# Two chunks' inner products of the SSD scan in one block on TensorE, and banks given by kind

## The chip, the cores and the metric

The kernel runs on one core of one Trainium2 chip. The metric is the device time of one execution in microseconds. Before the change three executions took 1362.30, 1364.81 and 1369.99 us; the median, 1364.81 us, is what the change is held against.

## The reference

One layer computes a gated merge of two branches: a chunked gMLP mixer and a Mamba-2 SSD mixer. The change touches only the SSD mixer. Cut to what matters, with 8 groups g of 4 heads r, chunks of 128 positions, a state of n = 128 and p = 64 channels to a head:

```python
cb     = einsum('bclgn,bcsgn->bcgls', cc, bc)
y_diag = einsum('bcgls,bcgrls,bcsgrp->bclgrp', cb, decay, xd)          # inside the chunk
states = einsum('bcsgn,bcgrs,bcsgrp->bcgrpn', bc, decay_to_end, xd)
state  = state * chunk_decay + states                                   # from chunk to chunk
y_off  = einsum('bclgn,bcgrpn,bcgrl->bclgrp', cc, prev_states, exp(a_cs))
y      = (y_diag + y_off + d_skip * x) * silu(z)
y_b    = rms_norm(y over the 256 columns of a group)
```

Around it stand a large product with `w_in` (all inputs of both branches), the products with `w_proj_a`, `w_proj_b` and `w_out`, and a last residual sum and norm. `decay` is the causal exp of sums of `dt * a`.

## The kernel before

The program has four stages: the modulation and the first columns, the products with `w_in` (to about 910 us of the profile), the SSD stage (about 910 to 1125 us), and then the products with `w_proj_b` and `w_out`. Large products run as seven half-size products with operands split in a high and a low part, type fp32r; what the SSD stage does itself is plain fp32.

The SSD stage works through 32 **steps**. A step is one group and two neighbouring chunks (256 positions); `order` lists them, two groups in turn: (0, s=0), (1, s=0), (0, s=1), (1, s=1) and so on up to s=3, then groups 2 and 3, and so on. Even steps belong to the first group of the two, odd ones to the second. For step n the methods of `Group` issue:

- `fetch`: two loads on the SP queue, `dcy` (the sums of `dt * a`, spread over partitions) and `sl` (B, C, x and z of the step).
- `mask` and `decay`: ACT makes `ea` from `dcy`, POOL masks `dcy`, ACT takes eight exps in `dcy`.
- `prep`: on TensorE (PE) two products `pc` = C·B, with transposes of B into the same bank, and four transposes of x into `px`; then on VectorE (DVE) `dcy * pc`, `xd` and `xe` from `px`; ACT copies `bn` out of `pc`.
- `front`: on PE eight **inner products** `yi` (the diagonal term: 64 columns of weights, 128 of data, each on one half of the array's columns), and one or two **state products** `sp`; on DVE the sum of state and `sp` (`st`), the two `y1` from `yi`, and for s < 3 a second `st`, which POOL prepares with `mul_state`.
- `back`: on PE `yn` (the state's term, two or four products); on DVE `ym` from it; on POOL the sum into `y1` and the product with the gate, `yz`.
- After each second step of a group the squares of `yz` are taken; a **strip**, `post2`, sums them over partitions: four products `pq` with 32 columns of weights each, whose result DVE turns into a row (`cwt` or `tri`) that goes to DRAM.

The product with `w_proj_a` (`proj_a`, tiles `pma`) is spread between the parts of a step: one `draw` is two matmuls of 128x512; DVE then makes `tha` from each finished pair of `pma` banks and `wal`, the low part of the next weights. Matmuls are pinned in program order; on DVE, ACT and POOL the chain `link` keeps the step's own work in program order, and a scheduler places the rest (`wal`, `tha`, the rows of the strips).

The loop before, for n from 2: `front(n)`, `ahead_of(n)` (decays of step n+3, `mul_state` of n+1, mask of n+4), a draw of 4 or 5, `back(n)`, `prep(n+2)`, `fetch(n+6)`. Strips that are due stand in `front` between `yi` and `sp`.

PSUM has eight banks: two under the tag `px`, six under `bk`. In this stage `bank(name)` gave every fourth tile a `px` bank, whatever it was. Two banks (four around the end of a block of `proj_a`) are held by `pma`.

Of the kernel before, what the change touches and what calls it, by code (L numbers as in the profile page):

```python
# [35 lines left out]
def hybrid_kernel(  # L36
# [53 lines left out]
    def load(dst, src):  # L90
        pin(nc.sync.dma_start(dst, src))
# [418 lines left out]
    def bank(name):  # L510

        if pairs_done:
            pairs_done.append(name)
            if len(pairs_done) % 4 == 2:
                return psum.tile([P, 512], F32, name=name, tag="px", bufs=2)
        return psum.tile([P, 512], F32, name=name, tag="bk", bufs=6)

# [51 lines left out]
    pending, pairs_done = [], []  # L569
# [519 lines left out]
    work, last, posts = [], {}, []  # L1089
# [19 lines left out]
    class Group:  # L1109


        def __init__(self, g):
            self.g, self.pre, self.st, self.yz, self.y = g, {}, None, {}, {}

        def fetch(self, s):
            g, nm = self.g, f"{self.g}_{s}"
            n = nstep[0] % NSET
            nstep[0] += 1
            pool, b = (p2r, 2) if n < 2 else (p2q, NSET - 2)
            dcy = pool.tile([P, HPG, 2, P], F32, name=f"dcy{nm}", tag="dcy", bufs=b)  # L1120
            load(dcy.rearrange("p h i l -> p (h i l)"),
                 acs_d[g, s].rearrange("h t -> (h t)").unsqueeze(0).to_broadcast([P, HPG * 256]))
            sl = pool.tile([P, 6, 256], F32, name=f"sl{nm}", tag="sl", bufs=b)
            load(sl, s_d[g][:, s])
            if n < 2:
# [44 lines left out]
            link("A", lambda: A.copy(bn, pc[:, 256:512]))  # L1170
            self.pre[s] = (sl, dcy, bn, xs[0], xs[1], ea)

        def front(self, s):

            g, nm = self.g, f"{self.g}_{s}"
            sl, dcy, bn, xd, xe, ea = self.pre[s]
            yi = bank(f"yi{nm}")
            for i in range(2):
                for h in range(HPG):
                    j, hh = h // 2, h % 2  # L1180
                    mm(yi[hh * HD : (hh + 1) * HD, j * 256 + i * P : j * 256 + (i + 1) * P],
                       xd[:, i * 256 + h * HD : i * 256 + (h + 1) * HD], dcy[:, h, i, :])
            while posts:
                p, q, sq = posts.pop(0)
                p.post2(q, sq)
            sp = bank(f"sp{nm}")
            two = s < NCH // 2 - 1
            self.sts = [self.st]
            for i in range(2 if two else 1):
                mm(sp[:, i * 256 : (i + 1) * 256], bn[:, i * P : (i + 1) * P], xe[:, i * 256 : (i + 1) * 256])  # L1190
            self.add_state(s, 0, sp)
            if two:
                self.mul_state(s, 1)
            y1 = turn(y1_r, f"y1{nm}", F32).rearrange("p (j t) -> p j t", j=2)
            for j in range(2):
                link("V", lambda: V.scalar_tensor_tensor(y1[:, j], sl[:, 2 + j], dskt[:, 2 * g + j : 2 * g + j + 1],
                                           yi[:, j * 256 : (j + 1) * 256], op0=ALU.mult, op1=ALU.add))
            self.y[s] = y1
            if two:
                self.add_state(s, 1, sp)  # L1200
# [333 lines left out]
    def draw(n):  # L1534
        for _ in range(n):
            left[0] -= next(fill, 1) is None
# [6 lines left out]
    def ahead_of(n):  # L1543

        with tc.high_priority():
            decays(n + 3)
            if n + 1 < len(order) and order[n + 1][1]:
                groups[order[n + 1][0]].mul_state(order[n + 1][1], 0)
            for _ in range(1 if n < 29 else 2):
                beside_step()  # L1550
            masks(n + 4)

    def step(n, *fs):
        for f in fs:
            item(getattr(groups[order[n][0]], f), order[n][1])

    draw(6)
    for n in range(2):
        step(n, "front")
        ahead_of(n)  # L1560
        draw(10)
    for n in range(len(order)):
        if n > 1:
            step(n, "front")
            ahead_of(n)
# [6 lines left out]
        fetch(n + 6)  # L1572
    while tasks or work or posts:
        draw(2)
        run_tasks()
        beside_step()
        while posts:
            p, q, sq = posts.pop(0)
            p.post2(q, sq)


    room.extend(ea_r[0] + [st_tag])
# [465 lines left out]
```

## Time and profile before

| | |
|---|---|
| three executions | 1362.30, 1364.81, 1369.99 us |
| span of the profiled execution, first to last instruction | 1361.7 us |
| PE busy | 1348.6 us (99%) |
| VectorE, ScalarE, GpSimd busy | 1053.0, 800.5, 195.0 us |
| SSD stage, steps | about 912 to 1112 us |

The profile is of one execution. The page gives its span and no separate time for what lies before the first and after the last instruction; the lowest of the three times is 0.6 us above this span, the median 3.1 us.

How to read the rows: a row of the timeline has start, duration, engine, line, operation, tiles (out<-in) and a count of equal instructions that follow each other; in brackets stands idle time before it and what ended it. One fp32 matmul of the program leaves two records, so eight `yi` are a row "x16". PEld is the loading of weights, which runs beside PE. The modelled ends of PE's rows overlap; what a block costs is read from the start of one to the start of the next.

### The profile page before, as it was taken

What the parts mean: (1) busy time and instruction counts of PE and PEld (TensorE: products, weight loads), DVE (VectorE), ACT (ScalarE), POOL (GpSimd) and SP (SyncE); (2) the same over time, 40 slices, a digit from 0 to 9 for tenths busy, and PEclk for the clock granted to TensorE, in tenths of its full rate; (3) what the DMA queues carried; (4) which work ended last, traced back from release to release, by engine and by line L of the source; (5) the groups of instructions that cost most, each with busy time, mean ns of one, the idle gap of its engine ahead of it and who ended that gap; (6) DMA issues with size and microseconds to landing.
All of it is one profiled execution on the core that took longest, in us unless ns stands there. A gap on an engine that the chain in (4) does not pass through costs nothing.

```text
span 1361.7 us, 20191 instructions
## 1 busy us (share of the span) xinstructions
PE 1348.6 (99%) x6943; PEld 1116.3 (82%) x6943; DVE 1053.0 (77%) x1728; ACT 800.5 (59%) x1449; POOL 195.0 (14%) x193
## 2 busy tenths in 40 slices
PE   8999999999999999999999999999999999999997
PEld 6688888888888888888888888888888888888886
DVE  4786886787777898688887788358888867959976
ACT  5763666666656665465566655486877844233443
POOL 1000000000000000000000000007798981000002
PEclk9999999999999999999999999999999999999999
DMA  9674444344345557877766765589989959888913
GB/s 279 190 244 132 147 124 124 104 129 123 94 139 155 172 188 225 257 224 235 215 193 188 241 207 184 160 289 311 307 297 314 306 199 333 317 268 319 384 40 124
DMA packets 249578, 288.65 MB, mean 212 GB/s; under 512 B 16860, under 2 KB 196484, under 8 KB 249476
## 3 DMA queue, kind: packets, MB, share of 16 engines
q1 hardware_dynamic: 174868, 203.80, 47.1%
q10 hardware_dynamic: 74544, 83.57, 17.9%
q8 instruction: 55, 0.90, 0.3%
q14 instruction: 47, 0.39, 0.1%
q0 software_dynamic: 64, 0.00, 0.0%
HBM read 199.82 MB, written 87.49 MB: 211 GB/s over the span
## 4 chain that ended last, share of the span: by engine, by line
PE 92%; DMA 4%; DVE 2%; SPq 1%; issue 0%; ACT 0%; POOL 0%; POOLq 0%; DVEq 0%; ACTq 0%
PE xcb L565 6%; PE xz L565 6%; PE xuz L565 6%; PE xx L565 6%; PE pma L82 6%; PE xg L565 6%; PE ox L1889 3%; PE yuz L565 3%; PE yx L565 3%; PE ycb L565 3%; PE vx L970 3%; PE yp L1697 3%; PE yz L565 3%; PE yg L565 3%; PE yi L82 2%; PE sp L82 2%
## 5 line engine op out<-in xcount | busy, mean ns | idle before, releaser
L1139 POOL TENSOR_SCALAR_AFFINE_SELECT dcy<-dcy 128x1024 f32<-128x1024 f32 x32 | 35.3, 1104 | 786.9 <-DMA yl<-ya_d 743.7
L1147 ACT ACTIVATE dcy<-dcy,nacs 128x128 f32<-128x128 f32 x256 | 78.3, 389 | 2.8 <-POOL dcy L1139 2.1
L1163 DVE TENSOR_TENSOR dcy<-dcy,pc 128x1024 f32<-128x1024 f32 x32 | 39.0, 1219 | 7.9 <-PE pc L85 6.4
L1245 POOL TENSOR_TENSOR yz<-y,sl 128x512 f32<-128x512 f32 x32 | 44.4, 1389 | 2.5
L82 PE MATMUL pma<-yh,wah 128*128 128x512 f32 x128 | 43.1, 418 | 0.0
L82 PE MATMUL pma<-yh,wal 128*128 128x512 f32 x128 | 42.6, 413 | 0.0
L1040 ACT ACTIVATE ac<-ac 128x1024 f32<-128x1024 f32 x32 | 33.9, 1060 | 12.7 <-DVE ac L1038 12.6
L82 PE MATMUL pma<-yl,wah 128*128 128x512 f32 x128 | 40.2, 395 | 0.0
L1135 ACT ACTIVATE ea<-dcy 64x512 f32<-64x512 f32 x64 | 39.8, 622 | 0.4
L1170 ACT COPY bn<-pc 128x256 f32<-128x256 f32 x32 | 11.9, 372 | 47.4 <-DVE dcy L1163 47.4
L1244 POOL TENSOR_TENSOR y<-y,ym 128x512 f32<-128x512 f32 (+1 forms) x32 | 37.0, 1157 | 2.1 <-DVE ym L1242 2.1
L1038 DVE SCALAR_TENSOR_TENSOR ac<-c2x,cwt,ac 128x1023 f32<-128x1023 f32 (+2 forms) x24 | 30.7, 1279 | 8.4 <-ACT ac L1036 8.3
L1038 DVE SCALAR_TENSOR_TENSOR ac<-c2cb,cwt,ac 128x1023 f32<-128x1023 f32 (+2 forms) x24 | 30.7, 1279 | 8.1 <-ACT ac L1036 7.9
L1632 DVE SCALAR_TENSOR_TENSOR yn<-yn,par,rb 128x512 f32<-128x512 f32 x32 | 24.5, 766 | 15.4 <-DMA yn<-yb_d 13.9
L1904 POOL TENSOR_TENSOR r<-r,fnw 128x512 f32<-128x512 f32 x4 | 6.1, 1530 | 204.1 <-ACT junk L1902 204.1
L82 PE MATMUL yi<-dcy,xd 128*64 128x128 f32 x512 | 35.0, 279 | 0.0
L1242 DVE TENSOR_TENSOR ym<-yn,ea 128x512 f32<-128x512 f32 (+1 forms) x32 | 19.9, 622 | 18.4 <-PE yn L82 18.3
L840 ACT CAST wbb<-wbr 128x512 fp32r<-128x512 f32 x32 | 19.8, 619 | 23.8 <-DMA wb_d<-wbb 17.4
L82 PE MATMUL sp<-xe,bn 128*128 128x256 f32 x112 | 32.7, 409 | 0.0
L82 PEld LDWEIGHTS yn<-sl,st 128*128 128x128 f32 x224 | 29.7, 191 | 2.9 <-POOL st L1208 0.4
L82 PEld LDWEIGHTS yi<-dcy,xd 128*64 128x64 f32 x512 | 27.3, 136 | 5.7 <-issue 3.2
L1038 DVE SCALAR_TENSOR_TENSOR ac<-c1cb,cwt,ac 128x1023 f32<-128x1023 f32 (+2 forms) x24 | 30.6, 1276 | 1.3 <-ACT ac L1036 1.3
(2978 smaller groups left out, 4379.1 us busy)
## 6 DMA issues: line engine op xcount, KB each, us to landing
sl<-s_d SPq DMA_DIRECT2D x32, 768.0 KB, 6.6
s_d<-ac ACTq DMA_DIRECT2D x32, 512.0 KB, 3.7
wb_d<-wbb ACTq DMA_DIRECT2D x32, 512.0 KB, 3.7
dcy<-acs_d SPq DMA_DIRECT2D x32, 512.0 KB, 5.0
av<-in_w_in_dram SPq DMA_DIRECT2D x36, 256.0 KB, 3.1
aw<-in_ada_w_dram SPq DMA_DIRECT2D x16, 512.0 KB, 5.9
wbr<-in_w_proj_b_dram SPq DMA_DIRECT2D x32, 256.0 KB, 4.8
yb_d<-yz ACTq DMA_DIRECT2D x32, 256.0 KB, 5.9
```

The source lines that it names most:

```text
L82: pin(PE.matmul(acc, l, r, start=first, stop=last))
L565: pin(PE.matmul(ps, lw[:, k * P : (k + 1) * P], r[k], start=first and n + k == 0, stop=n == 2 and k == 3, skip_group_check=not first))
L970: pin(PE.matmul(ps[pn][j], l[:, j * P : (j + 1) * P], r, start=nm in ("p1", "p5", "p2") and n + units[i][1] == 0, stop=n == 2 and k == 3, ...
L1038: V.scalar_tensor_tensor(ac[:, s:], cc[:, : S - s], conv_wt[:, 3 - s, i : i + 1], ac[:, s:], op0=ALU.mult, op1=ALU.add)
L1135: link("A", lambda: A.activation(ea[hh * HD : (hh + 1) * HD], dcy.rearrange("p (j e) i l -> p e j (i l)", e=2)[hh * HD : (hh + 1) * HD, hh ...
L1139: link("G", lambda: G.affine_select(out=d8, in_=d8, compare_op=ALU.is_ge, fill=-1e30, base=0, pattern=[[0, 2 * HPG], [1, P]], channel_mult ...
L1147: link("A", lambda: A.activation(dcy[:, h, i, :], dcy[:, h, i, :], AF.Exp, bias=sub[:, i, h : h + 1]))
L1163: link("V", lambda: V.tensor_tensor(d3, d3, pc[:, 0:256].unsqueeze(1).to_broadcast([P, HPG, 256]), op=ALU.mult))
L1244: link("G", lambda: G.tensor_add(y1[:, :, t0:], y1[:, :, t0:], m[:, :, t0:]))
L1245: link("G", lambda: G.tensor_mul(yz, y1, sl[:, 4:6]))
L1697: pin(PE.matmul(ps[j], a[:, v, js], r, start=first and n + k == 0, stop=n == 2 and k == KT - 1, skip_group_check=not first))
L1889: pin(PE.matmul(ps, a[:, tsl], b[:, cs], start=first and n + j == 0, stop=n == 2 and j == 3, skip_group_check=not first))
```

## The change

Three things are altered. The inner products become a method of their own, `inner`, and are issued for two steps at once: steps n and n+1 (n even) right before `front(n)`, behind a draw of 3; steps 0 and 1 stay single. The strips that are due stand right behind that block. The draws inside the loop become 3, 2 (3 for n=2) and 4 in place of 4 (6 for n=2) and 5. And the two `px` banks go to the tiles `px` and `pc` of `prep`, all else to the six others.

```diff
         if pairs_done:
             pairs_done.append(name)
-            if len(pairs_done) % 4 == 2:
+            if name[:2] in ("px", "pc"):
                 return psum.tile([P, 512], F32, name=name, tag="px", bufs=2)
         return psum.tile([P, 512], F32, name=name, tag="bk", bufs=6)
...
-        def front(self, s):
-
-            g, nm = self.g, f"{self.g}_{s}"
-            sl, dcy, bn, xd, xe, ea = self.pre[s]
-            yi = bank(f"yi{nm}")
+        def inner(self, s):
+
+            dcy, xd = self.pre[s][1], self.pre[s][3]
+            self.yi[s] = yi = bank(f"yi{self.g}_{s}")
             for i in range(2):
                 for h in range(HPG):
                     j, hh = h // 2, h % 2
                     mm(yi[hh * HD : (hh + 1) * HD, j * 256 + i * P : j * 256 + (i + 1) * P],
                        xd[:, i * 256 + h * HD : i * 256 + (h + 1) * HD], dcy[:, h, i, :])
-            while posts:
-                p, q, sq = posts.pop(0)
-                p.post2(q, sq)
+
+        def front(self, s):
+
+            g, nm = self.g, f"{self.g}_{s}"
+            sl, _, bn, _, xe, _ = self.pre[s]
+            yi = self.yi.pop(s)
             sp = bank(f"sp{nm}")
...
-    for n in range(len(order)):
-        if n > 1:
-            step(n, "front")
-            ahead_of(n)
-            draw(6 if n == 2 else 4 + n % 2)
+    def strips():
+        while posts:
+            p, q, sq = posts.pop(0)
+            p.post2(q, sq)
+
+    def inners(*ns):
+        with tc.high_priority():
+            for n in ns:
+                groups[order[n][0]].inner(order[n][1])
+            strips()
+
+    def behind(n):
         step(n, "back")
         if n == 1:
             draw(4)
         if n + 2 < len(order):
             step(n + 2, "prep")
         fetch(n + 6)
+
+    for n in range(2, len(order)):
+        if n % 2 == 0:
+            draw(3)
+            inners(n, n + 1)
+        step(n, "front")
+        ahead_of(n)
+        draw(4 if n % 2 else 3 if n == 2 else 2)
+        behind(n)
```

What it moves is seen best in the order of the instructions. First TensorE around steps 8 and 9 (groups 2 and 3, s=0; the names carry group and s). Before, from the transposes of step 9 through the inner products of step 8, one strip and the state product:

```order
L82 MATMUL yi2_0_9010<-dcy2_0_8685,xd2_0_8914 64x128 x8
L82 MATMUL pq1_0_9019<-yz1_0_8495,ones_140 32x128 x4
L82 MATMUL sp2_0_9026<-xe2_0_8916,bn2_0_8918 128x256 x2
L82 MATMUL pma2_0_8812<-yh30_8122,wal2_0_8563 128x512
L82 MATMUL pma2_1_8815<-yh31_8123,wal2_0_8563 128x512
```

In the changed kernel, the same place; six `pma` now stand between the transposes and this block:

```order
L82 MATMUL pma2_0_8812<-yh40_8141,wah2_1_8533 128x512
L82 MATMUL pma2_1_8815<-yh41_8142,wah2_1_8533 128x512
L82 MATMUL yi2_0_9009<-dcy2_0_8683,xd2_0_8923 64x128 x8
L82 MATMUL yi3_0_9018<-dcy3_0_8768,xd3_0_8990 64x128 x8
L82 MATMUL pq0_0_9027<-yz0_0_8465,ones_140 32x128 x4
L82 MATMUL pq1_0_9034<-yz1_0_8495,ones_140 32x128 x4
L82 MATMUL sp2_0_9041<-xe2_0_8925,bn2_0_8927 128x256 x2
```

The inner products of step 9 (`yi3_0`) have moved ahead of step 8's state product, and two strips that stood in two steps stand together.

Then VectorE, which takes its work in order, from `ym` of step 10 on. Before:

```order
L1242 TENSOR_TENSOR ym2_1_9210<-yn2_1_9205,ea2_1_8853 128x512
L1163 TENSOR_TENSOR dcy2_2_9005<-dcy2_2_9005,pc2_2_9217 128x1024
L1166 TENSOR_TENSOR xd2_2_9227<-px2_2_9216,dthq_154 128x512
L1166 TENSOR_TENSOR xe2_2_9229<-px2_2_9216,dde_155 128x512
L1400 TENSOR_TENSOR wal4_1_9381<-wa4_1_8808,wah4_1_9380 128x512
L1285 TENSOR_SCALAR cwt_148<-pq0_1_9247 128x128
L1216 TENSOR_TENSOR st_8275<-st_8275,sp3_1_9254 128x256
```

In the changed kernel:

```order
L1244 TENSOR_TENSOR ym2_1_9219<-yn2_1_9214,ea2_1_8851 128x512
L1402 TENSOR_TENSOR wal4_1_9334<-wa4_1_8808,wah4_1_9333 128x512
L1163 TENSOR_TENSOR dcy2_2_8996<-dcy2_2_8996,pc2_2_9226 128x1024
L1166 TENSOR_TENSOR xd2_2_9236<-px2_2_9225,dthq_154 128x512
L1166 TENSOR_TENSOR xe2_2_9238<-px2_2_9225,dde_155 128x512
L1218 TENSOR_TENSOR st_8275<-st_8275,sp3_1_9247 128x256
L1198 SCALAR_TENSOR_TENSOR y13_1_9252<-sl3_1_8931,dskt_151,yi3_1_9177 128x256 x2
```

Here `wal` has moved ahead of the next step's `dcy * pc`, and the strip's row has gone from this place.

Last, a piece of VectorE's order that reads the same in both: the work of step 5's `front` with the two `tha` of a finished block of `proj_a`, in the changed kernel:

```order
L1163 TENSOR_TENSOR dcy0_3_8525<-dcy0_3_8525,pc0_3_8750 128x1024
L1166 TENSOR_TENSOR xd0_3_8760<-px0_3_8749,dthq_154 128x512
L1166 TENSOR_TENSOR xe0_3_8762<-px0_3_8749,dde_155 128x512
L1218 TENSOR_TENSOR st_8275<-st_8275,sp1_2_8773 128x256
L1198 SCALAR_TENSOR_TENSOR y11_2_8778<-sl1_2_8489,dskt_151,yi1_2_8703 128x256 x2
L1508 SCALAR_TENSOR_TENSOR tha1_0_8452<-tha1_0_8452,pma1_0_8454 128x512
L1508 SCALAR_TENSOR_TENSOR tha1_1_8455<-tha1_1_8455,pma1_1_8457 128x512
L1218 TENSOR_TENSOR st22_8278<-st22_8278,sp1_2_8773 128x256
L1244 TENSOR_TENSOR ym1_2_8824<-yn1_2_8818,ea1_2_8491 128x512
L1163 TENSOR_TENSOR dcy1_3_8617<-dcy1_3_8617,pc1_3_8829 128x1024
```

What has moved against it is TensorE's order: before, the inner products of step 7, which read what the last row begins, stood behind those of step 6, a state product, five draws, `yn` and the transposes of step 8; now only three draws and the inner products of step 6 stand between.

More of the change, by code (lines that the diff above doesn't have):

```diff
@@ L1112, in __init__ @@
         def __init__(self, g):
-            self.g, self.pre, self.st, self.yz, self.y = g, {}, None, {}, {}
+            self.g, self.pre, self.st, self.yz, self.y, self.yi = g, {}, None, {}, {}, {}
         def fetch(self, s):
@@ L1555, in step @@
             item(getattr(groups[order[n][0]], f), order[n][1])
-    draw(6)
-    for n in range(2):
-        step(n, "front")
-        ahead_of(n)
-        draw(10)
-    for n in range(len(order)):
-        if n > 1:
-            step(n, "front")
-            ahead_of(n)
-            draw(6 if n == 2 else 4 + n % 2)
+    def strips():
[8 more added lines that the diff above has]
+    def behind(n):
         step(n, "back")
@@ L1572, in hybrid_kernel @@
         fetch(n + 6)
+    draw(6)
+    for n in range(2):
+        inners(n)
+        step(n, "front")
+        ahead_of(n)
+        draw(10)
+    for n in range(2):
+        behind(n)
[3 more added lines that the diff above has]
+            inners(n, n + 1)
+        step(n, "front")
+        ahead_of(n)
+        draw(4 if n % 2 else 3 if n == 2 else 2)
+        behind(n)
     while tasks or work or posts:
@@ L1576, in hybrid_kernel @@
         beside_step()
-        while posts:
-            p, q, sq = posts.pop(0)
-            p.post2(q, sq)
+        strips()
     room.extend(ea_r[0] + [st_tag])
```

## The prediction

> **What bounds the kernel now.** I read the page first: its head, the clock row and the chain that ended last.
>
> ```profile
> span 1361.7 us, 20191 instructions
> PE 1348.6 (99%) x6943; PEld 1116.3 (82%) x6943; DVE 1053.0 (77%) x1728; ACT 800.5 (59%) x1449; POOL 195.0 (14%) x193
> PEclk9999999999999999999999999999999999999999
> PE 92%; DMA 4%; DVE 2%; SPq 1%; issue 0%; ACT 0%; POOL 0%; POOLq 0%; DVEq 0%; ACTq 0%
> ```
>
> TensorE is busy 99% of the span at full clock, and 92% of the chain is TensorE. A busy PE can still hide gaps between blocks, so the stage of the change comes next: the view by windows for 930 to 1100 us (busy time of PE, PEld, DVE, ACT, POOL, then clock, DMA share and GB/s), and the view of waits in the same stretch.
>
> ```profile
> 930.00:1100.00 170.00, 170.00 (x1367) 144.87 (x1366) 143.26 (x253) 127.41 (x338) 147.22 (x143) 1.00 0.88 302
> ...
> DVE ym L1242 <- PE yn L82: 12.9, 17, 1.6
> DVE dcy L1163 <- PE pc L85: 5.7, 16, 0.5
> DVE st L1216 <- POOL st L1208: 5.7, 9, 1.3
> PEld sp L82 <- issue: 4.2, 23, 0.2
> PEld yi L82 <- issue: 2.4, 14, 0.2
> PEld pq L82 <- issue: 2.1, 12, 0.2
> ```
>
> No row there has PE waiting for another engine; VectorE waits for PE. POOL (147.22 of 170 us, 87%) and VectorE (143.26, 84%) are nearly full, though. The three last rows are the interesting ones: loading weights pauses 0.2 us for no engine, always at `yi`, `pq` and `sp`. The timeline of the weight loads shows where:
>
> ```profile
> 1010.53 0.85 PEld L82 LDWEIGHTS yi<-dcy,xd 128*64 128x64 f32 x16 [0.17 <-issue]
> 1011.55 0.16 PEld L82 LDWEIGHTS pq<-yz,ones 128*32 128x32 f32 x8 [0.17 <-issue]
> 1011.91 0.30 PEld L82 LDWEIGHTS sp<-xe,bn 128*128 128x128 f32 x2 [0.20 <-issue]
> ```
>
> The first shape of a row is the part of the array that the weights fill, and it changes at each pause: 128*128 to 128*64, to 128*32, and back. The next block waits there. The same place in PE's own timeline:
>
> ```profile
> 1008.44 1.05 PE L82 MATMUL yn<-sl,st 128*128 128x128 f32 x8
> 1009.33 0.39 PE L82 MATMUL pc<-sl 128*128 128x128 f32 x2
> ...
> 1010.22 0.38 PE L85 MATMUL px<-ident,sl 128*128 128x128 f32 x2
> 1010.53 1.09 PE L82 MATMUL yi<-dcy,xd 128*64 128x128 f32 x16
> 1011.55 0.43 PE L82 MATMUL pq<-yz,ones 128*32 128x128 f32 x8
> 1011.91 0.70 PE L82 MATMUL sp<-xe,bn 128*128 128x256 f32 x2
> ```
>
> From 1009.33 to 1010.22 eight records pass, 0.11 us each; two more end at 1010.44, and `yi` starts at 1010.53. **Entering costs 0.09 us.** Sixteen `yi` load in 0.85 us, yet `pq` starts 1.02 us after them. **Leaving costs 0.17 us.** A strip costs 0.36 us.
>
> **The change, part by part.** *Fewer entries.* Thirty steps come in 15 pairs with one entry and one exit each. `yi` is now entered from `pma` and not from `px`; the trace has that once, at step 0:
>
> ```profile
> 911.19 0.62 PE L82 MATMUL pma<-yl,wah 128*128 128x512 f32 x2
> 911.64 0.61 PE L82 MATMUL pma<-yh,wal 128*128 128x512 f32 x2
> 912.19 0.33 PE L82 MATMUL yi<-dcy,xd 128*64 128x128 f32 x2
> ```
>
> A pair of `pma` takes 0.45 us to the next, and 0.55 to `yi`: about 0.09 again. So each pair saves 0.09 + 0.17 = 0.26 us, and 15 x 0.26 = **3.9 us**. [...]
>
> *Strips together.* The order has 12 blocks of one strip in the loop before; now 4 blocks of two and 4 of one. Behind the loop the trace has two in one block:
>
> ```profile
> 1112.87 0.65 PE L82 MATMUL pq<-yz,ones 128*32 128x128 f32 x16
> 1113.44 0.50 PE L82 MATMUL pma<-yl,wah 128*128 128x512 f32 x1
> ```
>
> 0.57 us for two against 0.36 for one: the second costs 0.21, so 0.15 is saved four times, **0.6 us**. The gain on PE is 4.5 us. All else on PE is the same work in another place. `px` is now followed by `sp` at odd steps, same shape and type, at no cost.
>
> *What covers VectorE now.* Before, step n+1's `xd` had a whole step of PE work until its inner products. I lay out a pair by rows (n even, times in us from the end of the transposes of step n+1). The long leg: three draws 1.39, entry 0.09, `yi` of n at 1.48, **`yi` of n+1 at 2.33**, `sp` at 3.35. With
>
> ```profile
> 1023.68 1.13 PE L82 MATMUL sp<-xe,bn 128*128 128x256 f32 x4
> 1024.46 0.80 PE L82 MATMUL pma<-yh,wah 128*128 128x512 f32 x2
> 1025.10 0.63 PE L82 MATMUL pma<-yl,wah 128*128 128x512 f32 x2
> ```
>
> (`sp` 0.78, the first draw behind it 0.64) `yn` starts at 5.23, ends at 6.12, and the transposes of n+2 end at 7.23. The short leg from there: `sp` of n+1, four draws, `yn` from 2.81 to 3.70, transposes of n+3 until **4.81**. VectorE's part, from one step:
>
> ```profile
> 1000.93 0.41 DVE L1216 TENSOR_TENSOR st<-st,sp 128x256 f32<-128x256 f32 x1
> 1001.26 0.86 DVE L1196 SCALAR_TENSOR_TENSOR y<-sl,dskt,yi 128x256 f32<-128x256 f32 x2
> 1002.07 0.42 DVE L1216 TENSOR_TENSOR st<-st,sp 128x256 f32<-128x256 f32 x1
> 1004.04 0.69 DVE L1242 TENSOR_TENSOR ym<-yn,ea 128x512 f32<-128x512 f32 x1 [1.55 <-PE yn L82]
> 1004.98 1.22 DVE L1163 TENSOR_TENSOR dcy<-dcy,pc 128x1024 f32<-128x1024 f32 x1 [0.25 <-ACT ea L1135]
> 1006.12 0.68 DVE L1166 TENSOR_TENSOR xd<-px,dthq 128x512 f32<-128x512 f32 x1
> 1006.72 0.68 DVE L1166 TENSOR_TENSOR xe<-px,dde 128x512 f32<-128x512 f32 x1
> 1007.32 0.68 DVE L1400 TENSOR_TENSOR wal<-wa,wah 128x512 fp32r<-128x512 f32 x1
> 1007.91 0.41 DVE L1216 TENSOR_TENSOR st<-st,sp 128x256 f32<-128x256 f32 x1
> ```
>
> `dcy` starts about 0.04 behind the transposes and `xd` is done 1.82 later, at 1.86: **0.47 us ahead of the 2.33**, less the hand-over. In the short leg VectorE runs `dcy`, `xd`, `xe` until 2.38, `st` until 2.71, `y` until 3.52, `st` until 3.9, then `ym` behind `yn`, at 3.9, until 4.6; the next `dcy` is due at 4.85. So the common pair fits without a wait, with 0.25 us to spare on VectorE and some 0.3 more at `yi`. The bare cost is zero; the exceptions are:
>
> ```profile
> L1506 DVE SCALAR_TENSOR_TENSOR tha<-tha,pma x16: 673/678/687, 931.6 to 1129.7; 128x512 f32<-128x512 f32 x16
> ...
> L1285 DVE TENSOR_SCALAR cwt<-pq x8: 276/278/283, 964.1 to 1121.8; 128x128 f32<-128x128 f32 x8
> ```
>
> - Two short legs (steps 5 and 21) hold two `tha`: 1.2 us more, less 0.25 to spare, less 0.4 at `yi`: 0.5 us each, **1.0**. Behind them queue the second `st`, `ym` and `dcy`, and PE waits at the odd `yi`.
> - In the four blocks of two strips all six `bk` banks are taken (two `pma`, two `yi`, two `pq`), so `sp` needs one back: the first strip ends 0.43 us into its block, its row takes 0.28, and `sp` would stand at 0.57. With a hand-over 0.15 to 0.3 lost; I take 0.25, **1.0** in all.
> - In steps 10 and 26 two `tha` and a `wal` stand ahead of the next `dcy`, which comes 0.6 late; `st` of the odd step then ends behind 3.26, where the second half of `yn` needs it: 0.3 each, **0.6**.
> - Odd steps with s=0 need `st` at 2.81, and it ends at 2.79; with POOL's sums here and there, **0.4**.
>
> Together 3.0 us of new waits, with bounds of zero (VectorE hides it all) and 12 (0.8 in each of 15 pairs). I take 3.0, from the four places counted.
>
> *Banks by kind.* `px` and `pc` of one step now use the very banks of the step before; those come free with `xe`, 2.46 after the transposes, and ACT's `bn`, before that, and are needed at 3.70 at the earliest. Nothing, as long as VectorE is less than 1 us late.
>
> The stages behind are bound by PE and start that much earlier. The sum: 1361.7 - 4.5 + 3.0 = 1360.2 for this execution's span. The median stands 3.1 above that span and the lowest run 0.6, so I put the forecast between what the two give, 1360.8 and 1363.3, nearer the median: **1362.8 us**.
>
> **The rivals.**
>
> - *All of it is kept.* VectorE hides the exceptions as it hid them before. For: PE waits for nothing in 170 us now. Against: the cover was a step then and is 0.5 us now. 1364.8 - 4.5 = 1360.3.
> - *Slower: POOL and VectorE can't follow the short leg.* The second `st` of an odd step needs POOL's product with the state, which queues behind `y` and `yz` of the even step. The row above has VectorE waiting for it 9 times, once 1.3 us. That costs nothing now; where `dcy` comes over 0.5 us late it becomes a wait of PE at the odd `yi`. At 1.3 us late each pair loses 0.8: 15 x 0.8 - 4.5 = +7.5, 1372.3. For it speaks POOL's 87%; against it that the next long leg has 1.5 us in which VectorE catches up. [...]
> - *The gaps aren't the mode's.* If each new step's weights brought the pause, and not the change of shape, two `yi` blocks in a row would have it between them too: nothing saved, the waits stay, 1364.8 + 3.0 = 1367.8. Against it: the pauses stand at `pq` and `sp` too, always where the shape changes.
>
> **How the numbers follow.** Forecast 50%, all kept 20%, the short leg 18%, the gaps 12%. Two of the cases (70%) lie from 1360 to 1363, and the third run before was 5.2 above its median, so a median of few runs moves by some 2 us. The range, 1358.5 to 1370.0, takes in the first two cases, the gaps' and the milder half of the short leg. About 0.5%, 6.8 us, is what a measurement of this kernel can tell from no change. Faster than 1358.0 is more than PE's whole gain and needs a lucky median: 0.10. Slower than 1371.6 needs most of the short leg's price: 0.13. The rest, 0.77, is within it.
>
> **What would show it.** In the profile after: `yi` in rows of x32 with one pause ahead and one behind, 17 in place of 32; two strips in a row of x16 in the loop. Right in size, if SSD steps take 5 us less but for waits of PE at odd `yi`, at `sp` behind two strips and at `yn`, about 3 us together. Wrong, if PE waits at `yi` in most pairs (the short leg), or if `yi` x32 takes clearly over 1.87 us (the gaps).

## The result, and the profile after

| | before | changed |
|---|---|---|
| median (six executions each) | 1364.55 us | 1373.61 us |
| lowest, highest | 1362.30, 1369.99 us | 1372.13, 1376.82 us |
| span of the profiled execution | 1361.7 us | 1372.3 us |

The changed kernel is slower: the ratio is 1.0059, with a 95% interval of 1.0042 to 1.0076. The forecast of 1362.8 us and its range up to 1370.0 both missed. The medians differ by 9.1 us, the spans of the two profiled executions by 10.6; the rest of this text works with the spans, since only these executions have a trace.

The page of the changed kernel first, with the same lines that were shown of before.

```profile
span 1372.3 us, 20196 instructions
...
PE 1348.0 (98%) x6943; PEld 1115.7 (81%) x6943; DVE 1056.4 (77%) x1728; ACT 800.8 (58%) x1449; POOL 197.0 (14%) x193
...
PEclk9999999999999999999999999999999999999999
...
PE 82%; POOL 7%; issue 3%; DMA 3%; ACT 2%; SPq 1%; DVE 1%; POOLq 0%; ACTq 0%; DVEq 0%
```

PE is as busy in us as before, in a span that is 10.6 us longer: the time is idle time of PE, not more work. The chain that ended last agrees, since PE's share of it fell from 92% to 82%. Next the view by windows of 930 to 1100 us and, below it, PE's waits over the whole span (us in total, times, longest).

```profile
930.00:1100.00 170.00, 162.08 (x1290) 137.58 (x1290) 141.22 (x241) 121.30 (x321) 138.92 (x135) 1.00 0.84 288
```

```profile
PE pp L85 <- DMA pk<-in_ada_b_dram: 3.5, 1, 3.5
PE yn L82 <- DVE st L1218: 3.1, 4, 1.2
PE pq L82 <- POOL yz L1275: 1.9, 1, 1.9
PE yn L82 <- DVE y L1198: 1.5, 2, 0.8
PE yi L82 <- DVE xd L1166: 1.5, 1, 1.5
PE pma L82 <- DVE st L1218: 1.5, 1, 1.5
PE px L85 <- DVE x L359: 1.5, 2, 0.9
PE sp L82 <- DVE cwt L1287: 0.8, 4, 0.2
PE yi L82 <- ACT bn L1170: 0.6, 1, 0.6
PE yn L82 <- POOL st L1210: 0.6, 1, 0.6
```

Before, PE was busy for 170.00 of these 170 us and waited for nobody; now it is busy for 162.08. Most of its new waits name VectorE (8.4 us); 2.5 us name POOL and 0.6 ACT. Short ones do not appear as waits of PE, so I also read each block from its start to the start of the next and compared equal blocks with each other. Three starts cut the stage, and they can be read from PE's timeline: `yi` of step 4, `yi` of step 28, and the first product behind the stage, `x0p`. Before:

```profile
943.90 1.09 PE L82 MATMUL yi<-dcy,xd 128*64 128x128 f32 x16
...
1090.05 1.09 PE L82 MATMUL yi<-dcy,xd 128*64 128x128 f32 x16
...
1125.21 0.39 PE L1697 MATMUL x0p<-p1bh,p1a 128*128 128x512 f32 x1
```

The changed kernel, with its first `yi` at 911.71 (912.19 before):

```profile
911.71 1.09 PE L82 MATMUL yi<-dcy,xd 128*64 128x128 f32 x16
...
948.55 1.64 PE L82 MATMUL yi<-dcy,xd 128*64 128x128 f32 x26
...
1100.35 0.88 PE L82 MATMUL yi<-dcy,xd 128*64 128x128 f32 x12
...
1136.53 0.39 PE L1716 MATMUL x0p<-p1bh,p1a 128*128 128x512 f32 x1
```

The middle, steps 4 to 27, took 146.15 us and takes 151.80. The table has these stretches for every kernel of this study, from the first `yi` to `yi` of step 4, from there to `yi` of step 28, and from there to `x0p`. Where a pair stands at a cut, its draw ahead of the block moves a few `pma` records (0.23 us each) from one stretch to another; the numbers are put to the same count (74, 216 and 82). "Behind" is from `x0p` to the start of PE's last record.

| kernel | span | steps 0 to 3 | steps 4 to 27 | step 28 to `x0p` | behind |
|---|---|---|---|---|---|
| before | 1361.7 | 32.6 | 146.2 | 34.2 | 229.4 |
| changed | 1372.3 | 36.8 | 151.8 | 36.2 | 228.6 |
| e2_banks_alone | 1361.6 | 32.6 | 146.2 | 34.2 | 230.5 |
| e3_prep_behind | 1414.3 | 37.3 | 187.2 | 39.9 | 229.0 |
| e4_first_single | 1370.4 | 32.6 | 152.5 | 37.8 | 228.9 |
| e5_legs | 1372.0 | 37.2 | 150.8 | 36.5 | 228.8 |
| e6_sum_first | 1367.1 | 34.1 | 150.1 | 36.4 | 228.5 |
| e7_strip_banks | 1373.4 | 34.5 | 152.6 | 38.6 | 229.6 |
| e8_y_early | 1374.5 | 34.4 | 153.4 | 36.3 | 231.7 |
| e9_all | 1368.5 | 32.6 | 147.1 | 37.6 | 232.6 |
| e10_last_single | 1372.9 | 34.6 | 151.7 | 35.4 | 232.9 |
| e11_bn_behind | 1377.1 | 34.5 | 158.5 | 37.7 | 228.5 |
| e12_all_mid | 1373.0 | 32.7 | 154.8 | 37.7 | 229.6 |
| e13_all_y_late | 1376.3 | 34.1 | 156.7 | 36.9 | 230.3 |
| e14_quiet_pairs | 1364.7 | 32.6 | 146.5 | 34.3 | 233.4 |
| e15_sum_and_y | 1377.2 | 37.8 | 149.2 | 36.3 | 236.0 |
| e16_both_ends | 1364.8 | 32.6 | 147.6 | 35.2 | 231.0 |

So the 10.6 us are 4.2 at the start, 5.65 in the middle and 1.9 at the end, less 1.2 that other stages differ by. The waits themselves are larger, since the gain on PE is in these numbers: added up block by block they are 4.5, 10.4 and 2.5 us, 17.4 together, against a gain of 5.6. The middle's 10.4 are, by kind: 5.3 where an odd step's `yn` waits for the state sum `st`, 1.9 where `yn` of steps 5 and 21 waits for `y`, 1.9 at odd `yi`, 0.9 at `sp` behind strips, and 0.4 in pieces of 0.1 in blocks that began behind a wait.

The dearest place in the middle is step 11 (step 27 is its twin). This is the timeline of PE and VectorE there, with one row of POOL, from the second state sum of step 10 on.

```profile
990.86 0.41 DVE L1218 TENSOR_TENSOR st<-st,sp 128x256 f32<-128x256 f32 x1
...
991.19 0.68 DVE L1244 TENSOR_TENSOR ym<-yn,ea 128x512 f32<-128x512 f32 x1
991.21 1.03 PE L82 MATMUL sp<-xe,bn 128*128 128x256 f32 x4
991.42 1.09 POOL L1139 TENSOR_SCALAR_AFFINE_SELECT dcy<-dcy 128x1024 f32<-128x1024 f32 x1
991.79 1.26 DVE L1402 TENSOR_TENSOR wal<-wa,wah 128x512 fp32r<-128x512 f32 x1
...
992.98 1.21 DVE L1163 TENSOR_TENSOR dcy<-dcy,pc 128x1024 f32<-128x1024 f32 x1
...
993.91 0.60 PE L82 MATMUL yn<-sl,st 128*128 128x128 f32 x4
994.11 0.68 DVE L1166 TENSOR_TENSOR xd<-px,dthq 128x512 f32<-128x512 f32 x1
...
994.71 0.67 DVE L1166 TENSOR_TENSOR xe<-px,dde 128x512 f32<-128x512 f32 x1
995.31 0.41 DVE L1218 TENSOR_TENSOR st<-st,sp 128x256 f32<-128x256 f32 x1
...
995.76 0.71 PE L82 MATMUL yn<-sl,st 128*128 128x128 f32 x4 [1.25 <-DVE st L1218]
```

`sp` was done at about 992, and the sum that `yn` needs takes 0.41 us. But ahead of it in VectorE's queue stand `wal`, then `dcy`, `xd` and `xe` of step 12, whose inner products start only at 998.88. PE stands still for 1.25 us although VectorE is never idle: it works on what is not urgent.

### The profile page after: what moved, and what is told of

It is laid out like the page before. It is cut to its first block, busy times and chain, and to the rows that moved or that the text cites. A ratio compares the mean times of both kernels' runs of the same rounds, so it can differ in the third digit from the quotient of the medians.

```text
span 1372.3 us, 20196 instructions
## 1 busy us (share of the span) xinstructions
PE 1348.0 (98%) x6943; PEld 1115.7 (81%) x6943; DVE 1056.4 (77%) x1728; ACT 800.8 (58%) x1449; POOL 197.0 (14%) x193
## 4 chain that ended last, share of the span: by engine, by line
PE 82%; POOL 7%; issue 3%; DMA 3%; ACT 2%; SPq 1%; DVE 1%; POOLq 0%; ACTq 0%; DVEq 0%
PE xcb L565 6%; PE xz L565 6%; PE xuz L565 6%; PE xx L565 6%; PE xg L565 5%; PE ox L1908 3%; PE yuz L565 3%; PE yx L565 3%; PE ycb L565 3%; PE yz L565 3%; PE yp L1716 3%; PE vx L970 3%; PE yg L565 2%; PE oy L1908 2%; POOL y L1246 2%
## 5 line engine op out<-in xcount | busy, mean ns | idle before, releaser
L1139 POOL TENSOR_SCALAR_AFFINE_SELECT dcy<-dcy 128x1024 f32<-128x1024 f32 x32 | 37.8, 1182 | 784.2 <-DMA yl<-ya_d 743.7
L82 PE MATMUL pma<-yl,wah 128*128 128x512 f32 x128 | 44.1, 426 | 0.0
L1135 ACT ACTIVATE ea<-dcy 64x512 f32<-64x512 f32 x64 | 39.9, 623 | 0.6 <-DMA dcy<-acs_d 0.2
L1040 ACT ACTIVATE ac<-ac 128x1024 f32<-128x1024 f32 x32 | 33.9, 1061 | 10.8 <-DVE ac L1038 10.4
L82 PE MATMUL pma<-yh,wal 128*128 128x512 f32 x128 | 39.9, 393 | 0.0
L82 PE MATMUL yn<-sl,st 128*128 128x128 f32 x224 | 32.6, 281 | 5.6 <-DVE st L1218 3.1
```

The lines of the kernel that those rows point to most:

```text
L82: pin(PE.matmul(acc, l, r, start=first, stop=last))
L1135: link("A", lambda: A.activation(ea[hh * HD : (hh + 1) * HD], dcy.rearrange("p (j e) i l -> p e j (i l)", e=2)[hh * HD : (hh + 1) * HD, hh ...
L1139: link("G", lambda: G.affine_select(out=d8, in_=d8, compare_op=ALU.is_ge, fill=-1e30, base=0, pattern=[[0, 2 * HPG], [1, P]], channel_mult ...
```

## The experiments

The theories on record: S (the short leg, as the rival in the prediction had it), B (the banks), and from the fifth run on Q (the order in VectorE's queue), P (POOL and ACT), later A, T, L and M, each told where it is tested. Each run was one execution, but for e14. A single span is a loose measure, since 17 executions of the kernel before lie from 1361.42 to 1368.88 us; a stretch is a better one. The middle of the kernel before came out at 146.15 and 146.17 (e2), and that of the changed kernel, whose code from step 4 to step 27 is also that of e10 and e4, at 151.8, 151.7 and 152.5. So a difference of less than about 0.8 us in the middle says little.

**The banks alone.** The kernel before, with the new rule:

```diff
-            if len(pairs_done) % 4 == 2:
+            if name[:2] in ("px", "pc"):
```

> The kernel before with the banks given by kind, and nothing else of the change. Theory S (short leg: with the prep of step n+2 ahead of the front of step n+1 on VectorE, and little PE work between, PE waits for VectorE's st at the odd yn): inner products stay single, so no wait is new and the span stays at 1361.7 us, within 0.5. Theory B (banks: the six banks for all else are too few once pma holds four): PE waits 2.4 us at the first new block of proj_a, and 0.9 us at two later ones, as in the changed kernel: span 1364 to 1367 us.

Measured: span 1361.6 us, and every stretch of the stage equal to the kernel before within 0.1 us. Theory B falls: the bank rule costs nothing by itself, and the loss comes with the pairs and the strips that stand with them. A kernel with the pairs and the old rule was not run.

**The next step's preparation behind the odd step's front.**

```diff
-        if n + 2 < len(order):
+        if n + 2 < len(order) and (n < 2 or n % 2):
             step(n + 2, "prep")
...
         step(n, "front")
+        if n % 2 and n + 1 < len(order):
+            step(n + 1, "prep")
```

> The changed kernel, but for even n the prep of step n+2 is issued behind the front of step n+1, so that on VectorE st and y of the odd step stand ahead of dcy, xd and xe of step n+2. Theory S: the waits at odd yn (5.7 us in the changed kernel) and at odd yi (2.0 us) go for the most part: span 1365 to 1367 us. Theory B: the waits are for banks, the span stays at 1372 us, within 1.

Measured: 1414.3 us, a miss for both theories. The first two rows of PE's waits in that kernel, the second not a new one, say why:

```profile
PE pc L82 <- ACT bn L1170: 27.1, 11, 3.3
PE pp L85 <- DMA pk<-in_ada_b_dram: 3.5, 1, 3.5
```

The edit moved the transposes too, not only VectorE's work, so two preparations came close together and the second needed the two `px` banks while ACT had not yet emptied `pc`. It tested the banks, not the queue. The granted clock also fell nine times behind these waits, to 0.50, as told at the end.

**The first pair single, and other legs.** In e4 steps 2 and 3 are single, with draws of 6 and 4:

```diff
-        if n % 2 == 0:
+        if n < 4:
+            inners(n)
+        elif n % 2 == 0:
             draw(3)
             inners(n, n + 1)
...
-        draw(4 if n % 2 else 3 if n == 2 else 2)
+        draw(6 if n == 2 else 4 if n % 2 else 2)
```

> The changed kernel with steps 2 and 3 single as steps 0 and 1 are, pairs from step 4 on. Theory S: the 1.7 us wait at the inner products of step 3 goes, one pair's gain of 0.35 us goes too: span 1371 us. Theory B: that wait stays or moves to a bank: 1372 us or more.

In e5 one draw moves from ahead of the block into odd steps:

```diff
-            draw(3)
+            draw(2)
...
-        draw(4 if n % 2 else 3 if n == 2 else 2)
+        draw(5 if n % 2 else 3 if n == 2 else 2)
```

> The changed kernel with one draw moved from the long leg (2 in place of 3 ahead of the inner products) to the short leg (5 in place of 4). Theory S: the short leg is 0.46 us longer, which takes up to 0.46 off each wait at an odd yn (8 of them) and leaves the odd yi 0.46 less ahead of it: span 1369 to 1372 us, with the sum of the waits at yn down from 5.7 to about 3 us. Theory B: no change beyond 0.5 us.

Measured: e4 1370.4 us, near S's 1371, and e5 1372.0, which both theories allow. In e4 the first stretch is back at 32.6, all 4.2 us of it; the span fell by 1.9 only, since the middle and the end are longer there (how the end came to that is told at e9). What the pair of steps 2 and 3 ran into stands in the changed kernel's VectorE rows:

```profile
931.78 1.82 DVE L1402 TENSOR_TENSOR wal<-wa,wah 128x512 fp32r<-128x512 f32 x2
933.52 1.27 DVE L1508 SCALAR_TENSOR_TENSOR tha<-tha,pma 128x512 f32<-128x512 f32 x2
934.72 1.21 DVE L1163 TENSOR_TENSOR dcy<-dcy,pc 128x1024 f32<-128x1024 f32 x1
935.85 0.68 DVE L1166 TENSOR_TENSOR xd<-px,dthq 128x512 f32<-128x512 f32 x1
```

2.9 us of `proj_a`'s work stand ahead of step 3's `dcy`, and `yi` of step 3 waits until 936.59. The other 2.4 us of the start, steps 0 and 1, came with the execution and not with the change: kernels with the same code there (e7, e10, e11) have 34.5 us. The trace has the cause: POOL's first select of the stage took 3.52 us in the changed kernel and 3.51 in e15, the two with the whole of this loss, and 1.09 to 1.10 in the other fifteen kernels, the one before included; the 2.43 us between them are the loss (its row stands at the end of this text). e5 and e13 lose 1.2 and 1.5 us there behind a select of the usual length. In e5 the waits at odd `yn` shrink and odd `yi` waits in their place; to shift the draws only moves the wait.

**VectorE's order.** In e6 `xd` and `xe` of an even step (from step 4) are put aside in `prep` and issued by the odd step's `front` behind the first state sum:

```diff
             self.add_state(s, 0, sp)
+            while rest:
+                rest.pop(0)()
```

> The changed kernel, but on VectorE xd and xe of even steps (from step 4 on) stand behind the first state sum of the odd step before them; the rest of the order is kept. Theory Q (the order in VectorE's queue): the second half of yn of odd steps waits because the state sum stands behind dcy, xd and xe of the next step; with the sum 1.2 us earlier the waits at odd yn (5.7 us in all in the changed kernel) fall below 1.5 us, span 1372.3 - 4.2 = 1368.1, within 1. Theory P (POOL's products with the state and ACT's decays are what comes late): VectorE's order does not matter, the waits stay, span 1372.3 within 0.7.

In e7 strips use the `px` banks:

```diff
-            if name[:2] in ("px", "pc"):
+            if name[:2] in ("px", "pc", "pq"):
```

> The changed kernel, but strips take their banks from the two of px and pc. Both theories: the four waits of sp behind two strips (0.26 us each) go, and nothing else, since px and pc are free at that place: span 1372.3 - 1.1 = 1371.2, within 0.5. If the next transposes then wait for the rows of the strips, the span stays at 1372.3 or rises.

In e8 the `y` of a step is a method of its own, `diag`, and that of an odd step stands right behind the even step's front:

```diff
         step(n, "front")
+        if n % 2 == 0:
+            step(n + 1, "diag")
```

> The changed kernel, but the two y of an odd step (from step 3 on) stand on VectorE right behind the even step's front, and not in its own. Theory Q: the bank of odd yi comes free a step earlier, so yn of steps 5 and 21 no longer waits (-1.8 us); the short leg has 0.8 us less on VectorE, so dcy of the next step starts earlier and odd yi waits less (1.9 us now): span 1368.5 to 1369.5. Theory P: only the 1.8 us of the bank go, 1370.5.

e9 has these three edits and e4's.

> All of these together: single inner products for steps 2 and 3, xd and xe of even steps behind the odd step's first sum, y of odd steps early, strips in the banks of px and pc. Theory Q: 1372.3 - 1.9 - 4.2 - 1.1 - 1.8 - 1.0 = 1362.3, within 1.5, which is about the kernel before (1361.7 to 1362.7). Theory P: 1372.3 - 1.9 - 1.1 - 1.8 = 1367.5.

Measured: e6 1367.1, e7 1373.4, e8 1374.5, e9 1368.5 us. At step 11, e6 looks like this:

```profile
989.56 1.21 DVE L1165 TENSOR_TENSOR dcy<-dcy,pc 128x1024 f32<-128x1024 f32 x1
...
990.50 1.36 PE L82 MATMUL yn<-sl,st 128*128 128x128 f32 x8
990.69 0.41 DVE L1227 TENSOR_TENSOR st<-st,sp 128x256 f32<-128x256 f32 x1
991.02 0.68 DVE L1169 TENSOR_TENSOR xd<-px,dthq 128x512 f32<-128x512 f32 x1
991.62 0.67 DVE L1169 TENSOR_TENSOR xe<-px,dde 128x512 f32<-128x512 f32 x1
```

The sum comes ahead of `xd` and `xe`, and the eight records of `yn` pass in one row. In the middle the waits at odd `yn` for `st` fall from 5.3 to 0.65 us: the mechanism of theory Q is shown. But the middle got shorter by 1.7 us only, because 1.8 us come back at odd `yi` and 0.9 at the transposes, which wait for the later `xe`. Of e6's 5.2 us in the span, 2.7 stand in steps 0 to 3, mostly in what varies, so that the span came out near Q's 1368.1 in part by luck. In e7, where the span was to fall to 1371.2, no `sp` waits for a strip any more (0.9 us in the middle), yet the middle is 0.8 us longer and the end 2.5. In e8, which both theories had faster than the changed kernel, `yn` of steps 5 and 21 hardly waits any more (0.2 for 1.9), as both theories said, but the early `y` makes `ym`, the next `dcy` and the sum late, up to 2.1 us at step 11. Alone, e8 loses and e7 gains nothing; together (e9) the middle is 147.1 us, within 1 us of before.

The span of e9 does not follow, because of the end: it is nearer to P's 1367.5 than to Q's 1362.3, but for a reason that neither had. These are windows of e9 (the number ahead of the last two is PE's granted clock):

```profile
1114.00:1116.00 2.00, 1.41 (x12) 1.07 (x13) 1.44 (x1) 0.00 (x0) 1.92 (x3) 0.93 1.04 397
1116.00:1118.00 2.00, 2.00 (x6) 1.52 (x6) 0.53 (x2) 0.00 (x0) 2.00 (x2) 0.50 0.47 166
1118.00:1120.00 2.00, 2.00 (x8) 1.58 (x7) 0.00 (x0) 1.66 (x4) 1.12 (x2) 0.72 0.84 250
...
1134.00:1136.00 2.00, 2.00 (x6) 1.63 (x5) 2.00 (x4) 1.66 (x3) 0.69 (x1) 0.50 0.71 262
```

PE waited 2.03 us until 1114.59 for POOL's sum, as the changed kernel does for 1.9, and 1.9 us until 1131.5 for a strip's row. Behind both waits the granted clock fell to 0.50 for 3.4 us, which costs about 1.6 us each time (worked out at the end of this text). The same dip, to 0.50 for 3.4 us, lengthens the end of e4 (from 1121.1) and of e7 (from 1121.9).

**The end, and ACT.** In e10 steps 30 and 31 are single:

```diff
-        if n % 2 == 0:
+        if n > 29:
+            inners(n)
+        elif n % 2 == 0:
...
-        draw(4 if n % 2 else 3 if n == 2 else 2)
+        draw(4 + n % 2 if n > 29 else 4 if n % 2 else 3 if n == 2 else 2)
```

> The changed kernel, but steps 30 and 31 stay single, with the draws of before (4 and 5). Theory T (the end of the stage has its own price: the last step's sums and strips come later when step 31's front stands behind step 30's back with its inner products drawn ahead): the 2.1 us that PE waits at the strips behind the loop for POOL's sum go, less 0.35 for one pair's gain: span 1372.3 - 1.75 = 1370.5, within 0.5. If POOL is late from steps further back, the wait stays: 1372.6.

In e11 ACT's copy of `bn` of an even step (from step 4) is put aside in `prep` and issued behind the next decays:

```diff
             decays(n + 3)
+            while rest_b:
+                rest_b.pop(0)()
```

> The changed kernel, but ACT copies bn of an even step (from step 4 on) behind the decays of the odd step after it, and not ahead of them. Theory A (part of the lateness goes through ACT: bn waits for the bank that VectorE's dcy reads, the decays of the next step stand behind bn, and VectorE's next dcy waits for them): the waits at odd yi (1.95 us in all) go and those at odd yn, 5.7 us, do not grow: span 1372.3 - 2.0 = 1370.3, or lower. Theory Q alone (VectorE's queue): 1372.3 within 0.5.

e12 is e9 with both of these, and e13 is e12 without the early `y`.

> The kernel with all the edits of before together (single steps 2 and 3, state sum first, y of odd steps early, strips in the banks of px and pc), and now also steps 30 and 31 single and bn of even steps behind the decays. That kernel's stage took 217.3 us against 213.0 of the kernel before, with 3.9 us of waits at the strips and late squares behind the loop, 2.3 at odd yi and 2.3 behind the stage for a row of strips. If each wait has its own cause: 1368.5 - 3.9 - 2.3 - 2.3 = 1360.0, 1 to 2 us below the kernel before. If the waits only move on: 1364 to 1367.

> The same, but with y of odd steps in their own front again. Steps 5 and 21 then wait for their bank at yn as in the changed kernel: +1.8 us against the run before it in this job. If the early y costs as much elsewhere (its run alone was 2.2 us slower than the changed kernel), the two are equal or this one is faster.

Measured: e10 1372.9, e11 1377.1, e12 1373.0, e13 1376.3 us. In e10 the stretch at the end falls by 0.8 us (the wait for POOL's sum from 1.9 to 0.8), less than half of what theory T said, and a wait of 2.5 us for the last `tha` appears behind the stage, with a dip of the clock to 0.50. Theory A falls as a remedy: with `bn` later, PE waits at the transposes for its bank (4.9 us for `px` in e11), and e12 and e13 carry the same stall. As e3 did, it shows that the two `px` banks have to be emptied soon. Its mechanism is borne out, though: in e11 VectorE's `dcy` nowhere waits for ACT's exps any more, and the waits at `yi` of steps 11, 27 and 31 are gone (more on this in the next section). e12 missed both of its numbers by 6 us or more, and e12 and e13 do not test what they were made for. Between them e13 was to be 1.8 us slower or equal; its middle is 2.0 us longer and its span 3.3.

**Where pairs are cheap, and which edits belong together.**

In e14 six pairs are left:

```diff
-        if n % 2 == 0:
+        if n & -2 not in (8, 12, 14, 16, 24, 28):
+            inners(n)
+        elif n % 2 == 0:
...
-        draw(4 if n % 2 else 3 if n == 2 else 2)
+        draw(6 if n == 2 else 4 + n % 2 if n & -2 not in (8, 12, 14, 16, 24, 28) else 4 if n % 2 else 2)
```

> The changed kernel, but pairs only for steps 8, 12, 14, 16, 24 and 28 and their followers, where the changed kernel's PE waited least; all others single with the draws of before (6 for n=2, else 4 and 5). Theory L (each pair pays its own waits, set by what else VectorE holds at that place; a pair there does not disturb the steps around it): six pairs gain 6 x 0.35 = 2.1 us and two double strips 0.3, against waits of 0.27 twice, 0.15 three times and 0.44 once: 1361.7 - 1.0 = 1360.7 within 1, and the stage up to the last step about 1 us shorter than before. Theory M (POOL, ACT and VectorE are late on the whole; any pair brings waits, in the mean 0.82 a pair as in the changed kernel's steps 4 to 27): 1361.7 + 6 x 0.47 = 1364.5.

e15 has the edits of e6 and e8 alone, and e16 is e9 with steps 30 and 31 single.

> The changed kernel with two edits alone: xd and xe of even steps behind the odd step's first state sum, and y of odd steps early. From the inner products of step 4 to those of step 28 the kernel before takes 146.15 us, the changed kernel 151.80, the sum alone 150.06, the early y alone 153.40, and all edits together 147.1. Theory Q (VectorE's order, the two edits need each other: y has left the short leg, so that the state sum and dcy both come early): 147.5 to 148.5 in that stretch. If the strips' banks did it: 150 or more.

> All edits together as before (single steps 2 and 3, sum first, early y, strips in the banks of px and pc), and steps 30 and 31 single, without the edit of bn. Theory T (the end has its own price): the stretch from step 28 to the first product behind the stage falls from 37.6 to 35.4 us, and the span to 1368.5 - 2.2 = 1366.3; to 1363 if PE's clock does not fall behind the waits at the end either.

Measured, e14: median 1367.58 us of 12 executions against 1363.95 of 17 before, a ratio of 1.0029 with an interval of 1.0017 to 1.0040; span 1364.7. The span is M's number (1364.5), but by luck: in the stage, where M would have some 3 us more than before and L about 1 less, the middle is 146.5 us, 0.3 longer than before, and the other two stretches are as before. The waits that L listed are there again, 0.15 at steps 9, 17 and 25 and 0.45 at steps 14 and 15, and so are local to a pair's place, as L has it (these pairs bring no two strips together, so neither that gain nor those waits of L's sum come up); but even the cheap places no more than pay for themselves, since single strips now wait for POOL's sums (0.4 us at step 11). The other 4 us lie behind the stage, at a place whose code is the same in both kernels, here in PE's timeline:

```profile
1125.36 0.39 PE L1718 MATMUL x1p<-p1bh,p1a 128*128 128x512 f32 x1
1128.71 0.50 PE L1718 MATMUL x2p<-p1bh,p1a 128*128 128x512 f32 x1 [2.96 <-DVE tha L1508]
```

The bank of `x2p` was still held by `proj_a`'s last block; in the kernel before, `x2p` follows at once. Which bank falls to it seems to depend on how the banks were given out; I did not test this.

e15: the middle is 149.2 us, between the two answers. Its span of 1377.2 us, the longest but for e3's, has two other sources: the slow select at the start again, with a dip of the clock behind it (0.50 for 3.4 us), and a wait of 4.76 us at `x2p` with another (0.50 for 6.8 us), by which the part behind the stage is 6.6 us longer than before. In the middle the two edits bring 2.6 us of the 5.65, and e16, which adds the strips' banks and the ends, 1.5 more. e16 is the best of the full versions with 1364.8 us; its last stretch fell by 2.4 us, as theory T said, and the span by 3.7. No version came out below the kernel before; e16's one execution (1366.82 us) lies within the scatter of that kernel.

## Why the prediction failed, step by step

- **Fewer entries (3.9 us) and strips (0.6): right in mechanism, a little small.** The gain was 5.6 us in the stage where 4.5 was forecast. A clean pair shows it: in e9, from `yi` of step 4 to that of step 6, nothing waits:

```profile
944.06 1.97 PE L82 MATMUL yi<-dcy,xd 128*64 128x128 f32 x32
...
956.02 1.20 PE L82 MATMUL yi<-dcy,xd 128*64 128x128 f32 x18
```

That is 11.96 us. Before, from the row at 943.90 to this one, it was 12.30:

```profile
956.20 0.98 PE L82 MATMUL yi<-dcy,xd 128*64 128x128 f32 x14
```

So a pair saves 0.34 where 0.26 was forecast, 5.1 us in 15 pairs, and the four double strips bring the rest; `sp` of odd steps, now behind transposes, takes 0.68 us to the next block and not 0.78, which the working had not seen. The rival that the gaps come with each new step's weights, and not with the change of shape, falls: the 32 records pass in one row (at 944.06) with no pause between the two steps.

- **"The common pair fits without a wait": this step failed.** The working gave `st` of an odd step the end 2.71 against a need at 3.26, half a microsecond of room. It laid out one pair, with VectorE's work in a row with nothing between, at its shortest durations. Three things are not in it:
  - At s=3 (steps 7, 15 and 23) `sp` is half as long, 0.25 us and not 0.68, so `yn` comes 0.43 earlier. `dcy` starts only 0.1 us later than in other pairs there (0.5 behind step 23), and yet `yn` waits 0.3 to 0.7 for `st`.
  - At steps 3 and 19 a `wal` stands ahead of the next `dcy`, as at the listed steps 11 and 27; `dcy` starts 0.6 to 0.7 us later than in other pairs, and `yn` waits 0.4 and 0.5.
  - Odd `yi` waits in six of the later pairs, 0.07 to 0.9. In five of them (steps 11, 15, 19, 27 and 31) VectorE stood idle for 0.3 to 0.95 us ahead of `dcy`, 3.4 us together, for ACT's exps, which it does nowhere in the kernel before. In ACT's order the exps of the odd step stand behind the even step's `bn` and two squares, and `bn` waits for the even step's `dcy`, which reads the same bank. At step 11 (the `dcy` of step 10 runs from 979.19 for 1.22 us):

```profile
980.45 0.37 ACT L1170 COPY bn<-pc 128x256 f32<-128x256 f32 x1 [3.33 <-DVE dcy L1163]
980.85 1.15 ACT L1271 ACTIVATE yz<-yz 128x512 f32<-128x512 f32 x2
981.90 2.44 ACT L1147 ACTIVATE dcy<-dcy,nacs 128x128 f32<-128x128 f32 x8
...
984.37 1.22 DVE L1163 TENSOR_TENSOR dcy<-dcy,pc 128x1024 f32<-128x1024 f32 x1 [0.95 <-ACT dcy L1147]
```

The rival "short leg" came nearest, with 7.5 us more than the median before where 9.1 were measured, but not by its path: PE waits most at odd `yn`, for a sum that is ready to run but queued, it waits at odd `yi` in 7 of the 15 pairs, in five of these behind ACT, and only 0.6 us of its waits at `yn` name POOL's product.

- **The four places.** Strips: 0.27 each, as said (0.25). Odd steps with s=0: 0.15 in each of three, 0.45 where 0.4 was said. Steps 5 and 21: right place, 0.93 for 0.5, and another cause: four banks are held by `pma` there, `yi` and `sp` hold the other two, and `yn` needs the one that `y` frees. Steps 11 and 27: right mechanism, `wal` ahead of `dcy`, but 1.51 each where 0.3 was taken; `wal` took 1.26 us and not 0.68.
- **Banks by kind "nothing": right alone** (e2), though with pairs in flight the six banks are what the waits at strips and at steps 5 and 21 come from (e7 and e8 take these two away).
- **The ends were not in the sum at all.** 4.2 us at steps 0 to 3 (of which 2.4 are the slow select, in this execution) and 1.9 at the end: the working laid out one pair of the middle and multiplied it, and looked for exceptions only there.
- **From span to time: a little off.** The executions of this study that have both on record are 1.8 to 2.1 us longer than their span; the 0.6 and 3.1 in the working held times and span of different executions against each other. This moves the forecast by less than 1 us.

In one line: in the stage a gain of 4.5 us and 3.0 us of waits were forecast, 5.6 and 17.4 were measured, and the term that was mis-sized is the new waits.

Shown by a run are: what the pair of steps 2 and 3 costs (e4), the queue order behind the waits at odd `yn` (e6), the bank behind steps 5 and 21 (e8) and behind the strips (e7), ACT's order behind the waits at `yi` of steps 11, 27 and 31 (e11), and that waits belong to places (e14). Not settled is why the edits help only together, why the first select is slow in some executions, and what decides the bank of `x2p`.

## What to carry to other kernels

A saving on the bounding engine that works by bunching also bunches its suppliers' deadlines, here with 5.6 us gained and 17.4 us of waits: lay out the suppliers' queues for every place of the loop, first and last rounds included, with the durations they have beside their neighbours (`wal` took 0.68 us and 1.26), before counting the saving. An engine with idle time left can still be late, when what is urgent stands behind what is not (VectorE is busy for 77% of the changed kernel's span, and PE waits 1.25 us for its sum at step 11); look at the order in its queue before adding cover. And check one edit by the stretch it touches as well as by the span: here e2 repeats each stretch of the stage before within 0.1 us, while what comes behind the stage moved the span of other kernels by up to 6.6 (e15).

## What the runs showed of the hardware

- PE's clock fell at some short waits and not at others. Behind or within waits of 1.5 to 5.1 us the granted clock was 0.50 for about 3.4 us (twice that in three cases, one each in e3, e11 and e15), in e4, e5, e7, e9 (twice), e10 to e15, and nine times in e3; after others as long (1.89 in the changed kernel, 2.67 in e8) it stayed at 1.00. In e9 the two dips begin at 1115.72 and 1132.79 and last 3.41 us each. In the second, nine records of 128x512 take 3.65 us, from 1132.75 to 1136.40; nine take 2.04 at 1.00, from 1138.02 to 1140.06. The difference is the 1.6 us put down for a dip, an estimate for the others. What decided which waits brought a dip was not shown.
- VectorE's and POOL's operations took longer beside each other. `wal` took 0.68 us in the prediction's row and 1.26 beside POOL's select (the rows at 991.42 and 991.79): it started 0.37 us behind the select and ended at 993.05, 0.54 behind the select's end. The mean of its 16 was 0.92 us before and 1.14 after. Of the 20 that stand alone in a row, in the two kernels together, 15 began while a POOL operation had more than 0.3 us to run, and took 0.93 to 1.75 us; the other five took 0.68 or 0.69. At the start a select took 3.52 us, not 1.09:

```profile
915.62 3.52 POOL L1139 TENSOR_SCALAR_AFFINE_SELECT dcy<-dcy 128x1024 f32<-128x1024 f32 x1 [18.63 <-ACT ea L1135]
...
915.69 2.50 DVE L1380 TENSOR_TENSOR yl<-yl,yh 128x512 fp32r<-128x512 f32 x4
```

It ended at 919.14, 0.95 us behind VectorE's four operations. In the kernel before, the select there took 1.09 us (from 916.09) and the four operations 3.36 (from 916.17), where they took 3.52 and 2.50 here. The select's row starts 0.07 us ahead of theirs in the changed kernel and 0.08 before; what decided which of the two took longer, no run here shows.
